# Layer 0's output begun inside the delta rule's last rounds, with GpSimd in the written order and shorter chains of the output norms

## The chip, the cores and the metric

The kernel runs on one core of a Trainium2 chip. The metric is the device time of one execution in microseconds (us). A core has five engines that work side by side: TensorE (PE in the profile; its weight loads are PEld), VectorE (DVE), ScalarE (ACT), GpSimd (POOL) and SyncE (SP), which starts most transfers. Each works through its own instructions in order and waits at an instruction for semaphores that others raise.

## The reference

The program is a backbone of two layers over 256 context rows and 512 latent rows of width 1024. Layer 0 is a gated DeltaNet in both directions, layer 1 an attention layer. The change concerns the end of layer 0. The delta rule goes through chunks of 64 rows:

```python
def step(s, xs):
    qk_i, qd_i, kd_i, u_i, w_i, gl_i = xs
    v_new = u_i - jnp.einsum('bhcd,bhde->bhce', w_i, s)
    o = jnp.einsum('bhcd,bhde->bhce', qd_i, s) + jnp.einsum('bhcs,bhse->bhce', qk_i, v_new)
    s = s * gl_i[..., None, None] + jnp.einsum('bhcd,bhce->bhde', kd_i, v_new)
    return s, o
```

and its output o (16 heads of 128) is normed, gated and multiplied with the output weights:

```python
def finish(o, z):
    b, h, l, dv = o.shape
    o = rms_norm(jnp.transpose(o, (0, 2, 1, 3)), o_norm_g).astype(z.dtype)
    return (o.reshape(b, l, DN_VAL_DIM) * jax.nn.silu(z)) @ w_out
```

A gated residual add follows, then layer 1, which begins with a norm of the rows h.

## The kernel before, in words

All 768 rows are six tiles of 128 (t = 0 to 5); O[t] holds the delta rule's output of a tile for 16 heads.

**The loop.** The delta rule is a loop of 50 rounds x over 48 updates: x // 4 is a step along the chunks, x % 4 a set of four heads. Round x issues products(x) (TensorE ks, L1065; VectorE r, L1068; ScalarE o, L1070; GpSimd's decay of the state S, L1073, twice, and on a tile's second visit its O += o, L1076), solve(x-1) (pr, L1090, and ScalarE's vn, L1092) and update(x-2) (pq, L1112; su, L1120; VectorE's O +=, L1123, and S +=). So three updates are on their way at any time. Steps before the last one make su; the last four updates (44 to 47) don't.

**The norms of O.** square_o (L896, ScalarE) sums the squares of a tile and head. scale_pieces is a generator: each send issues two or three small VectorE operations (L906 to L926) that make 1/sqrt with a corner of a PSUM bank as scratch, and its last pieces scale O by fo on GpSimd, four operations a tile (L932). In the loop the scratch is a corner of pq or a tile "room"; the generators for tiles 0 and 1 start at round 24, for tile 5 at 39.

**The output.** 32 units n (two groups of three tiles, 16 heads each). Unit n+2 is prepared while unit n is multiplied: three transposes of O into the PSUM tile pt (L980), the gate (L983, VectorE, times silu z), ScalarE's copy y0 = pt rounded (L985), VectorE's y1 = pt - y0 (L986). Then po of unit n: 18 matmuls, three tiles by two halves by three passes, y0 x woh, y0 x wol, y1 x woh (L1205). The output weights wo come by a transfer and are split in woh (ScalarE, L947) and wol = wo - woh (first half GpSimd L949, second half VectorE L951). There are two buffers for woh and wol, so the cast for unit n+2 waits for the last matmul of unit n. In units 0 to 9 ScalarE also squares O of tiles 4, 3 and 2 (five a unit), and the generators for these tiles start at units 4, 7 and 10, four sends a unit, behind the copy, with column 3 of pt as scratch.

**Behind group 0.** gated (L1214, VectorE) multiplies the accumulators by a gate; GpSimd adds the results to h (L1221) and ScalarE squares h (L1222), two each in units 16, 17 and 18. norms1 makes their 1/sqrt in unit 20 and normed (L1246, ScalarE) scales h in units 21 to 23. From unit 24 on u_block turns h for layer 1: transposes ht (L1255), one VectorE operation (L1257), ScalarE's copy and VectorE's difference uC (L1258, L1259). pt and ht share two PSUM banks, "tr".

**The order.** PE, DVE and ACT run in the order in which the program issues them (tc.manual_schedule). GpSimd is not in that list in the loop and the units, and a scheduler places its instructions. PSUM has eight banks: in the loop two each for ks, pr, pq and su; behind it two for "tr" and six for the accumulators.

Of the kernel before, what the change touches and what calls it, by code (L numbers as in the profile page):

```python
# [8 lines left out]
F32 = mybir.dt.float32  # L9
# [8 lines left out]
P = 128  # L18
# [79 lines left out]
def backbone(tc, a, out):  # L98
# [799 lines left out]
    def scale_pieces(t0, n):  # L898


        c = n * VH
        f, o_, y, w = (x[:, t0:t0 + n].rearrange("p t h -> p (t h)") for x in (fo, oss, oy, ow))
        r_ = rq[:, t0:t0 + n].rearrange("p t h -> p (t h)")
        by2 = lambda x: x.rearrange("p (h r) -> p h r", r=2)
        sp = (yield)[:, 0:c]
        V.tensor_copy(sp, o_)  # L906
        V.tensor_tensor(by2(sp), by2(sp), bcast(r_, 2, 2), ALU.mult)
        V.tensor_copy(w, sp)
        sp = (yield)[:, 0:c]
        V.tensor_copy(sp, w)  # L910
# [15 lines left out]
        V.tensor_tensor(by2(f), by2(sp), bcast(r_, 2, 2), ALU.mult)  # L926
        for t in range(t0, t0 + n):
            for q in range(4):
                if q % 2 == 0:
                    yield  # L930
                h = slice(4 * q, 4 * q + 4)
                G.tensor_tensor(O[t][:, h], O[t][:, h], bcast(fo[:, t, h], 2, P), ALU.mult)  # L932

# [38 lines left out]

    def out_y(n, pt=None):

        gi, h = units0[n]
        z = zs.pop(n)
        if pt is None:
            pt = ptr.tile([P, 4, P], F32, tag="tr", name=f"pt{h}_{gi}")
        for j, (t, off, st_) in enumerate(GROUPS[gi]):
            T.transpose(pt[:, j, :], O[t][:, h, :], ident)  # L980
        for j, (t, off, st_) in enumerate(GROUPS[gi]):
            pj = pt[:, j].rearrange("p (a k) -> p a k", a=2)
            V.scalar_tensor_tensor(pj, pj, og, raw(z, off, [[st_, 2], [1, 64]]), ALU.mult, ALU.mult)  # L983
        y = [fw.tile([P, 3, P], F32R, tag=f"y{i}", name=f"y{i}_{h}_{gi}", bufs=3) for i in range(2)]
        S.copy(y[0], pt[:, :3])  # L985
        V.tensor_tensor(y[1], pt[:, :3], y[0], ALU.subtract)  # L986
        ys[n] = y
        return pt

    with tc.tile_pool(name="psC", bufs=2, space=PSUM, reuse_waits="tile") as pcx:  # L990
# [59 lines left out]
        def products(x):  # L1050
# [8 lines left out]
            for j in range(2):  # L1059
                hh = 2 * p + j  # L1060
                ks = pcx.tile([P, 2, 2, P], F32, tag="ks", name=f"ks{x}_{j}", bufs=2)
                for w in range(2):
                    for d in range(2):
                        r0 = (visit ^ d) * 64
                        T.matmul(ks[r0:r0 + 64, w], kq[:, w, slot(hh), r0:r0 + 64], St[hh][:, d], start=True, stop=True)  # L1065
                h0 = 2 * slot(hh)
                for i in range(2):
                    V.scalar_tensor_tensor(r[:, 2 * j + i], ks[:, 0, i], negV[:, visit, t, h0 + i:h0 + i + 1], v[:, 2 * hh + i], ALU.mult, ALU.add)  # L1068
                for i in range(2):
                    S.activation(o[:, 2 * j + i], ks[:, 1, i], AF.Copy, scale=egV[:, visit, t, h0 + i:h0 + i + 1])  # L1070
                if s < 11:
                    g_ = glb[:, visit, :, t, h0:h0 + 2]
                    G.tensor_tensor(St[hh], St[hh], bcast(g_, 3, P), ALU.mult)  # L1073
# [27 lines left out]
        def update(x):  # L1101
# [11 lines left out]
            if s < 11:  # L1113
                su = pcx.tile([P, 2, 2, 2, P], F32, tag="su", name=f"su{x}", bufs=1)
# [29 lines left out]
        for _, g_ in chores:  # L1144
            next(g_)
        with tc.manual_schedule(engines={T.engine, V.engine, S.engine}):
            for x in range(50):
                if x < 48:
                    products(x)
                if 0 <= x - 1 < 48:  # L1150
                    solve(x - 1)
                if x == 49:
                    for h in range(2):
                        out_y(h, pcx.tile([P, 4, P], F32, tag="ks", name=f"pt{h}_0", bufs=2))
                if 0 <= x - 2 < 48:
# [5 lines left out]
                if x in (45, 46):  # L1161
                    out_load(x - 45)
                    out_weights(x - 45, False)
                    out_z(x - 45)
        for _, g_ in chores:
            for _ in g_:
                pass

    ch_c.__exit__(None, None, None)


    tr_c = tc.tile_pool(name="psT", bufs=2, space=PSUM, reuse_waits="tile")
    ptr = tr_c.__enter__()
    PASS = ((0, 0), (0, 1), (1, 0))
    SCALE = 128.0 ** -0.5
# [20 lines left out]
    ORDER = [t for g_ in GROUPS for t, _, _ in g_]  # L1196

    def products0(n, acc):

        gi, h = units0[n]  # L1200
        y, ww = ys.pop(n), weights.pop(n)
        for j in range(3):
            for nh in range(2):
                for x, (i, k) in enumerate(PASS):
                    T.matmul(acc[j][nh], y[i][:, j, :], ww[k][:, nh * 512:(nh + 1) * 512], start=h == 0 and x == 0, stop=h == VH - 1 and x == 2)  # L1205

# [29 lines left out]
    def norms1(gi, room_):  # L1236
# [12 lines left out]

    def u_block(k, j, tiles, dst):  # L1250

# [7 lines left out]
        V.tensor_tensor(dst[1][:, k], pv, dst[0][:, k], ALU.subtract)  # L1259
# [7 lines left out]
    for g_ in chores.values():  # L1267
        next(g_)
    squares = [(t, h) for t in (4, 3, 2) for h in range(VH)]
    late_adds = []  # L1270
    loads0 = {3: lambda: load_h(0), 5: lambda: load_h(1), 7: lambda: load_h(5), 9: lambda: dma(gate0[:, 0], gate_d[0][:, 0]), 11: lambda: dma(gate0[:, 1], gate_d[0][:, 1]), 13: lambda: load_h(4), 18: lambda: load_h(3), 20: lambda: load_h(2)}
    for n in range(len(units0)):
        gi, h = units0[n]
        if h == 0:
            acc = [[pf.tile([P, 512], F32, tag=f"po{j}{nh}", name=f"po{gi}{j}{nh}") for nh in range(2)] for j in range(3)]
# [508 lines left out]
```

## Time and profile before

| what | us |
|---|---|
| three runs of the kernel, median | 1248.55 |
| lowest and highest of them | 1247.85, 1249.84 |
| the profiled execution, whole time | 1247.08 |
| its span (first to last instruction) | 1245.3 |
| mean granted clock of TensorE | 0.977 |
| the delta rule's last products begin | 773.72 |
| first matmul of the output (po) | 783.48 |
| group 0's last unit ends, about | 862.7 |
| first transposes of h (ht) | 903.71 |

A row of the trace in order of time reads: start, duration, engine, line, operation, output <- inputs with their shapes, how many in a row (x8), and in brackets how long the engine was idle before it and what ended that. A row of a window reads: its bounds and length, the busy time of each engine (and instructions), the granted clock, the busy share of the DMA engines and GB/s. The line numbers are those of the kernel before; the profile calls a buffer by its name without the number.

### The profile page before, as it was taken

What the parts mean: (1) busy time and instruction counts of PE and PEld (TensorE: products, weight loads), DVE (VectorE), ACT (ScalarE), POOL (GpSimd) and SP (SyncE); (2) the same over time, 40 slices, a digit from 0 to 9 for tenths busy, and PEclk for the clock granted to TensorE, in tenths of its full rate; (3) what the DMA queues carried; (4) which work ended last, traced back from release to release, by engine and by line L of the source; (5) the groups of instructions that cost most, each with busy time, mean ns of one, the idle gap of its engine ahead of it and who ended that gap; (6) DMA issues with size and microseconds to landing.
All of it is one profiled execution on the core that took longest, in us unless ns stands there. A gap on an engine that the chain in (4) does not pass through costs nothing.

```text
span 1245.3 us, 28148 instructions
## 1 busy us (share of the span) xinstructions
PE 1151.1 (92%) x10755; PEld 925.9 (74%) x10755; DVE 833.3 (67%) x1884; ACT 724.4 (58%) x1934; POOL 601.2 (48%) x486
## 2 busy tenths in 40 slices
PE   3999999999789979899999999889999989999896
PEld 1776778888678868788666666768777778989784
DVE  2498666868688655575688888577666766556535
ACT  4544346665575767974689887543543246766621
POOL 0121123149999999700485598347455043140630
PEclk9999999999899989999999999999999999999998
DMA  9478965555435589555978855456744011111133
GB/s 316 159 222 268 297 216 165 149 143 187 127 98 158 175 247 273 191 193 184 274 213 241 236 159 156 159 170 194 208 161 136 18 51 52 35 34 52 59 103 93
DMA packets 165496, 204.56 MB, mean 164 GB/s; under 512 B 13393, under 2 KB 114930, under 8 KB 164594
## 3 DMA queue, kind: packets, MB, share of 16 engines
q1 hardware_dynamic: 146162, 193.10, 50.7%
q10 hardware_dynamic: 19200, 9.67, 2.6%
q8 instruction: 85, 1.39, 0.5%
q14 instruction: 49, 0.40, 0.1%
HBM read 161.96 MB, written 40.67 MB: 163 GB/s over the span
## 4 chain that ended last, share of the span: by engine, by line
PE 55%; DVE 13%; POOL 11%; ACT 7%; DMA 6%; issue 5%; SPq 2%; ACTq 0%; POOLq 0%; DVEq 0%
PE ks L1065 7%; PE g_z L414 6%; PE g_k L414 4%; PE g_q L414 4%; PE po L1205 4%; POOL X L755 4%; POOL tmp L754 3%; PE pg L1488 3%; PE su L1120 3%; PE po L1597 2%; PE pr L1090 2%; PE pso L1616 2%; PE pg L1534 2%; PE pa L245 2%; PE pq L1112 2%
## 5 line engine op out<-in xcount | busy, mean ns | idle before, releaser
L1073 POOL TENSOR_TENSOR S<-S,glb 128x512 f32<-128x512 f32 x88 | 90.1, 1046 | 112.8 <-PE ks L1065 112.6
L1205 PE MATMUL po<-woh,y 128*128 128x512 f32 x384 | 128.3, 402 | 1.0 <-DVE O L1123 0.8
L414 PE MATMUL g_v<-uh,wh 128*128 128x512 f32 (+1 forms) x256 | 91.2, 356 | 15.8 <-DVE sil_v L441 15.8
L755 POOL TENSOR_TENSOR X<-X,tmp 128x62 f32<-128x62 f32 (+15 forms) x93 | 95.7, 1029 | 6.5
L436 DVE SCALAR_TENSOR_TENSOR acc_v<-g_v,cwv,acc_v 128x510 f32<-128x510 f32 (+3 forms) x128 | 74.5, 609 | 33.4 <-ACT acc_v L433 32.0
L1065 PE MATMUL ks<-S,ckq 128*64 128x256 f32 x768 | 93.5, 385 | 3.1 <-ACT o L1070 2.5
L754 POOL TENSOR_TENSOR tmp<-L,X 128x62 f32<-128x62 f32 (+15 forms) x93 | 89.9, 967 | 6.9
L414 PE MATMUL g_z<-uh,wh 128*128 128x512 f32 (+1 forms) x256 | 88.4, 345 | 4.4 <-DVE sil_v L441 4.4
L414 PE MATMUL g_v<-ul,wh 128*128 128x512 f32 (+1 forms) x256 | 89.9, 351 | 0.0
L414 PE MATMUL g_v<-uh,wl 128*128 128x512 f32 (+1 forms) x256 | 89.2, 349 | 0.0
L414 PE MATMUL g_z<-ul,wh 128*128 128x512 f32 (+1 forms) x256 | 86.9, 340 | 0.0
L414 PE MATMUL g_z<-uh,wl 128*128 128x512 f32 (+1 forms) x256 | 86.8, 339 | 0.0
L949 POOL TENSOR_TENSOR wol<-wo,woh 128x512 fp32r<-128x512 f32 (+1 forms) x32 | 53.4, 1671 | 68.6 <-ACT woh L947 63.9
L1205 PEld LDWEIGHTS po<-woh,y 128*128 128x128 f32 x384 | 72.9, 190 | 16.4 <-DVE O L1123 1.2
L1205 PE MATMUL po<-wol,y 128*128 128x512 f32 x192 | 76.1, 396 | 7.6 <-POOL wol L949 7.6
L1065 PEld LDWEIGHTS ks<-S,ckq 128*64 128x64 f32 x768 | 50.7, 136 | 42.2 <-ACT o L1070 11.3
L211 POOL TENSOR_TENSOR wl_k<-w_k,wh_k 128x1024 fp32r<-128x1024 f32 x8 | 19.2, 2402 | 100.4 <-ACT wh_k L210 100.4
L414 PEld LDWEIGHTS g_v<-uh,wh 128*128 128x128 f32 x256 | 50.8, 198 | 22.6 <-DVE sil_v L441 16.5
L1580 DVE TENSOR_TENSOR pT<-pt,pT 128x384 fp32r<-128x384 f32 x64 | 33.3, 554 | 42.3 <-ACT pT L1579 42.3
L1138 DVE TENSOR_TENSOR S<-su,S 128x512 f32<-128x512 f32 x88 | 56.5, 684 | 4.3 <-PE su L1120 3.0
L1068 DVE SCALAR_TENSOR_TENSOR r<-ks,negV,cv 128x128 f32<-128x128 f32 x192 | 56.2, 344 | 4.1 <-PE ks L1065 3.3
L414 PEld LDWEIGHTS g_z<-uh,wh 128*128 128x128 f32 x256 | 48.9, 191 | 10.4 <-DVE sil_v L441 5.3
(417 smaller groups left out, 3378.0 us busy)
## 6 DMA issues: line engine op xcount, KB each, us to landing
aw<-in_ada_w SPq DMA_DIRECT2D x24, 1024.0 KB, 7.8
w<-in_dn_w_in SPq DMA_DIRECT2D x40, 512.0 KB, 4.4
wo<-in_dn_w_out SPq DMA_DIRECT2D x32, 512.0 KB, 3.5
cv<-v_d SPq DMA_DIRECT2D x80, 128.0 KB, 5.3
df<-gc_d SPq DMA_DIRECT2D x48, 128.0 KB, 2.8
z_d<-zs SPq DMA_DIRECT2D x16, 384.0 KB, 5.1
v_d<-vt ACTq DMA_DIRECT2D x16, 384.0 KB, 4.4
t_d<-Tt SPq DMA_DIRECT2D x6, 1024.0 KB, 5.1
```

Source lines behind the costliest of these rows:

```text
L414: mm = T.matmul(pg_[:m, :n], w[:, k, :m], u[:, k, c0:c0 + n], start=k == 0 and n_ == 0, stop=k == KT - 1 and n_ == 2)
L436: V.scalar_tensor_tensor(acc[:, c0 + lo:c0 + hi], ps[:, lo + j - 2:hi + j - 2], cwv[:, j, ct:ct + 1], acc[:, c0 + lo:c0 + hi], ALU.mult, A ...
L754: E.tensor_tensor(tv, bcast(L[:, :, j + 1:, j], 3, j + 1), bcast(X[:, :, j, 0:j + 1], 2, n), ALU.mult)
L755: E.tensor_tensor(X[:, :, j + 1:, 0:j + 1], X[:, :, j + 1:, 0:j + 1], tv, ALU.subtract)
L949: G.tensor_tensor(wl[:, :c], w[:, :c], wh[:, :c], ALU.subtract)
L1065: T.matmul(ks[r0:r0 + 64, w], kq[:, w, slot(hh), r0:r0 + 64], St[hh][:, d], start=True, stop=True)
L1068: V.scalar_tensor_tensor(r[:, 2 * j + i], ks[:, 0, i], negV[:, visit, t, h0 + i:h0 + i + 1], v[:, 2 * hh + i], ALU.mult, ALU.add)
L1073: G.tensor_tensor(St[hh], St[hh], bcast(g_, 3, P), ALU.mult)
L1120: T.matmul(su[c0:c0 + 64, d ^ j, j], kt[r0:r0 + 64, 4 * j + p, c0:c0 + 64], vd[r0:r0 + 64, 2 * j:2 * j + 2], start=True, stop=True)
L1138: V.tensor_tensor(St[hh], raw(sj, 0, [[512 - 1024 * j, 2], [P, 2], [1, P]]), St[hh], ALU.add)
L1205: T.matmul(acc[j][nh], y[i][:, j, :], ww[k][:, nh * 512:(nh + 1) * 512], start=h == 0 and x == 0, stop=h == VH - 1 and x == 2)
L1488: T.matmul(pgq, uL[i][:, k, t * P:(t + 1) * P], wq[j][:, k], start=k == 0 and n_ == 0, stop=k == KT - 1 and n_ == 2)
```

## The change

Four things. The lines of the changed kernel are other numbers for the same statements (L929 the scaling of O, L947 wol, L1102 O += o, L1242 the addition to h).

1. The generators of the norms issue 16 small operations in place of 27, in 5 sends in place of 12. Their scalings are put on a list, and scale_o(n) issues the next n of it at written places: one or two in nine of the rounds 30 to 47, then one behind the weights of each unit, two from unit 12 on.
2. GpSimd joins the written order in the loop and the units.
3. ks moves into the pool of pt ("tr"), and su, the scratch tile and the accumulators of a group's first tile share another. So unit 0's transposes and gate stand in round 48 ahead of the last solve, unit 1's behind update(46), and the first tile's six matmuls of units 0 and 1 behind the last update. The weights of the first two units are loaded two rounds earlier and split one round earlier or at the same place.
4. out_y and u_block are split in two. In the units with small operations, these (two sends a unit) now stand between gate and copy; in the units from 24 on the transposes of pt and ht stand together, then both VectorE operations, then copy and difference of each. norms1 for group 0 becomes a generator in units 19 and 20.

The diff, cut:

```diff
@@ scale_pieces
-                if q % 2 == 0:
-                    yield
-                h = slice(4 * q, 4 * q + 4)
-                G.tensor_tensor(O[t][:, h], O[t][:, h], bcast(fo[:, t, h], 2, P), ALU.mult)
+                pool_todo.append((t, q))
+
+    def scale_o(n):
+        for t, q in pool_todo[:n]:
+            h = slice(4 * q, 4 * q + 4)
+            G.tensor_tensor(O[t][:, h], O[t][:, h], bcast(fo[:, t, h], 2, P), ALU.mult)
+        del pool_todo[:n]
...
@@ the loop
-        with tc.manual_schedule(engines={T.engine, V.engine, S.engine}):
+        with tc.manual_schedule(engines={T.engine, V.engine, S.engine, G.engine}):
             for x in range(50):
                 if x < 48:
                     products(x)
+                if x == 48:
+                    out_first(0)
                 if 0 <= x - 1 < 48:
                     solve(x - 1)
-                if x == 49:
-                    for h in range(2):
-                        out_y(h, pcx.tile([P, 4, P], F32, tag="ks", name=f"pt{h}_0", bufs=2))
                 if 0 <= x - 2 < 48:
                     update(x - 2)
+                if x == 48:
+                    out_second(0)
+                    out_first(1)
+                if x == 49:
+                    out_second(1)
+                    acc0 = first_acc(0)
+                    for n in range(2):
+                        products0(n, [acc0], (0,))
...
+                scale_o({30: 2, 31: 2, 34: 1, 37: 1, 40: 1, 43: 1, 45: 1, 46: 2, 47: 1}.get(x, 0))
...
@@ the units
-        pt = out_y(n + 2) if n + 2 < len(units0) else None
+        pt = out_first(n + 2) if n + 2 < len(units0) else None
+        if n >= 24:
+            u_first(n - 24, 1, (0, 1))
+        if n == 19:
+            next(chores[19])
         for x in [x for x in chores if x <= n]:
-            for _ in range(4):
+            for _ in range(2):
                 try:
                     chores[x].send(pt[:, 3])
...
+        if n + 2 < len(units0):
+            out_second(n + 2)
+        if n >= 24:
+            u_second(n - 24, 1, uC)
...
-        products0(n, acc)
+        products0(n, acc, (1, 2) if n < 2 else (0, 1, 2))
...
         if n + 2 < len(units0):
             out_weights(n + 2)
+        scale_o(2 if n >= 12 else 1)
         if n in (16, 17, 18):
             for x in range(2):
                 added(*late_adds.pop(0), G)
```

GpSimd from the weights of unit 13 to those of unit 20, before (wol_0 is group 0, wol_1 group 1, which begins with unit 16; O_7091 and O_7090 are tiles 3 and 2; L1221 is the addition to h):

```order
L949 TENSOR_TENSOR wol_0_10926<-wo_0_10834,woh_0_10925 128x512
L949 TENSOR_TENSOR wol_0_10974<-wo_0_10883,woh_0_10973 128x512
L932 TENSOR_TENSOR O_7090<-O_7090,fo 128x512 x4
L949 TENSOR_TENSOR wol_0_11015<-wo_0_10933,woh_0_11014 128x512
L949 TENSOR_TENSOR wol_1_11054<-wo_1_10981,woh_1_11053 128x512
L1221 TENSOR_TENSOR h_10296<-h_10296,gy_0_11092 128x512
L949 TENSOR_TENSOR wol_1_11105<-wo_1_11022,woh_1_11104 128x512
L1221 TENSOR_TENSOR h_10296<-h_10296,gy_1_11094 128x512
L1221 TENSOR_TENSOR h_10297<-h_10297,gy_0_11096 128x512
...
L949 TENSOR_TENSOR wol_1_11150<-wo_1_11061,woh_1_11149 128x512
L949 TENSOR_TENSOR wol_1_11193<-wo_1_11118,woh_1_11192 128x512
```

The same place now:

```order
L929 TENSOR_TENSOR O_7091<-O_7091,fo 128x512 x2
L947 TENSOR_TENSOR wol_0_10966<-wo_0_10887,woh_0_10965 128x512
L929 TENSOR_TENSOR O_7090<-O_7090,fo 128x512 x2
L947 TENSOR_TENSOR wol_1_11007<-wo_1_10932,woh_1_11006 128x512
L929 TENSOR_TENSOR O_7090<-O_7090,fo 128x512 x2
L947 TENSOR_TENSOR wol_1_11060<-wo_1_10975,woh_1_11059 128x512
L947 TENSOR_TENSOR wol_1_11104<-wo_1_11016,woh_1_11103 128x512
L1242 TENSOR_TENSOR h_10292<-h_10292,gy_0_11047 128x512
L1242 TENSOR_TENSOR h_10292<-h_10292,gy_1_11049 128x512
L947 TENSOR_TENSOR wol_1_11147<-wo_1_11072,woh_1_11146 128x512
L1242 TENSOR_TENSOR h_10293<-h_10293,gy_0_11051 128x512
L1242 TENSOR_TENSOR h_10293<-h_10293,gy_1_11053 128x512
```

The scalings of tile 2 stood as four ahead of wol of unit 15 and now stand as two behind it and two behind that of unit 16. The first addition to h stood behind wol of unit 16 and five more behind that of unit 17; now two stand behind wol of 18, 19 and 20 each.

VectorE in unit 4, where the norm of tile 4 begins, before (unit 6 is prepared; pt_0_10511 is its tile):

```order
L983 SCALAR_TENSOR_TENSOR pt_0_10511<-pt_0_10511,og,z_0_10460 128x128 x3
L986 TENSOR_TENSOR y_6_0_10519<-pt_0_10511,y_6_0_10518 128x384
L906 COPY pt_0_10511<-oss 128x16
L907 TENSOR_TENSOR pt_0_10511<-pt_0_10511,rq 128x16
...
L919 TENSOR_TENSOR ow<-pt_0_10511,oy 128x16
L951 TENSOR_TENSOR wol_0_10556<-wo_0_10463,woh_0_10555 128x512
```

And now:

```order
L982 SCALAR_TENSOR_TENSOR pt_0_10493<-pt_0_10493,og,z_0_10442 128x128 x3
L906 TENSOR_TENSOR pt_0_10493<-oss,rq 128x16
L907 TENSOR_TENSOR pt_0_10493<-pt_0_10493,rq 128x16
L908 TENSOR_SCALAR fo<-pt_0_10493 128x16
L910 COPY pt_0_10493<-fo 128x16
L911 TENSOR_SCALAR pt_0_10493<-pt_0_10493 128x16
L912 TENSOR_SCALAR oy<-pt_0_10493 128x16
L992 TENSOR_TENSOR y_6_0_10507<-pt_0_10493,y_6_0_10506 128x384
L949 TENSOR_TENSOR wol_0_10534<-wo_0_10445,woh_0_10533 128x512
```

Ten small operations stood behind the difference y1; now six stand between the gate and y1, and so ahead of ScalarE's copy, which y1 needs.

TensorE at the end of the loop now (pr and pq belong to the last solves and updates; pt_0_10216 and pt_0_10248 are units 0 and 1):

```order
L1138 MATMUL pq_10204<-vn_10153,cQK_9976 64x128 x8
L979 MATMUL pt_0_10216<-ident,O_7088 128x128
L979 MATMUL pt_0_10216<-ident,O_7089 128x128
L979 MATMUL pt_0_10216<-ident,O_7093 128x128
L1116 MATMUL pr_10223<-r_10172,cT_9975 64x128 x8
L1138 MATMUL pq_10234<-vn_10202,cQK_9976 64x128 x8
L979 MATMUL pt_0_10248<-ident,O_7088 128x128
...
L1138 MATMUL pq_10255<-vn_10232,cQK_9976 64x128 x8
L1004 MATMUL po_10269<-woh_0_10060,y_0_0_10244 128x512
```

Before, both units' transposes stood between the last two pq, and the first po behind unit 2's transposes.

More of the change, by code (lines that the diff above doesn't have):

```diff
@@ L987, in out_y, with products0, first_acc @@
         ys[n] = y
-        return pt
+    PASS = ((0, 0), (0, 1), (1, 0))
+    def products0(n, acc, js):
+        gi, h = units0[n]
+        y, ww = ys[n], weights[n]
+        for j in js:
+            for nh in range(2):
+                for x, (i, k) in enumerate(PASS):
+                    T.matmul(acc[j][nh], y[i][:, j, :], ww[k][:, nh * 512:(nh + 1) * 512], start=h == 0 and x == 0, stop=h == VH - 1 and x == 2)
+    tr_c = tc.tile_pool(name="psT", bufs=2, space=PSUM, reuse_waits="tile")
+    ptr = tr_c.__enter__()
+    psU_c = tc.tile_pool(name="psU", bufs=1, space=PSUM, reuse_waits="tile")
+    pU = psU_c.__enter__()
+    def first_acc(gi):
+        x = pU.tile([P, 2, 512], F32, tag="su", name=f"po{gi}0")
+        return [x[:, nh] for nh in range(2)]
     with tc.tile_pool(name="psC", bufs=2, space=PSUM, reuse_waits="tile") as pcx:
@@ L1060, in products @@
                 hh = 2 * p + j
-                ks = pcx.tile([P, 2, 2, P], F32, tag="ks", name=f"ks{x}_{j}", bufs=2)
+                ks = ptr.tile([P, 2, 2, P], F32, tag="tr", name=f"ks{x}_{j}")
                 for w in range(2):
@@ L1113, in update @@
             if s < 11:
-                su = pcx.tile([P, 2, 2, 2, P], F32, tag="su", name=f"su{x}", bufs=1)
+                su = pU.tile([P, 2, 2, 2, P], F32, tag="su", name=f"su{x}")
                 for j in range(2):
@@ L1160, in backbone @@
                         squares = squares[1:]
[L1161 to L1167, printed above, removed]
+                scale_o({30: 2, 31: 2, 34: 1, 37: 1, 40: 1, 43: 1, 45: 1, 46: 2, 47: 1}.get(x, 0))
+                if x in (43, 45):
+                    out_load((x - 43) // 2)
+                    out_z((x - 43) // 2)
+                if x in (44, 46):
+                    out_weights((x - 44) // 2, False)
+        assert not chores and not pool_todo, (chores, pool_todo)
     ch_c.__exit__(None, None, None)
-    tr_c = tc.tile_pool(name="psT", bufs=2, space=PSUM, reuse_waits="tile")
-    ptr = tr_c.__enter__()
-    PASS = ((0, 0), (0, 1), (1, 0))
     SCALE = 128.0 ** -0.5
@@ L1196, in backbone @@
     ORDER = [t for g_ in GROUPS for t, _, _ in g_]
[L1198 to L1205, printed above, removed]
     def gated(gi, acc):
@@ L1240, in norms1, with norm_pieces @@
         rsqrt(r, 1.0 / D, room=room_)
+    def norm_pieces(gi):
+        r = hr[:, 3 * gi:3 * gi + 3]
+        y = hpool.tile([P, 3], F32, tag="hy", name=f"hy{gi}")
+        V.tensor_tensor(r, hsq[:, 3 * gi:3 * gi + 3, 0], hsq[:, 3 * gi:3 * gi + 3, 1], ALU.add)
+        sp = (yield)[:, 0:3]
+        V.tensor_scalar(sp, r, 1.0 / D, EPS, ALU.mult, ALU.add)
+        V.tensor_copy(r, sp)
+        V.tensor_single_scalar(sp.bitcast(I32), sp.bitcast(I32), 1, ALU.logical_shift_right)
+        V.tensor_scalar(y.bitcast(I32), sp.bitcast(I32), -1.0, float(0x5F3759DF), ALU.mult, ALU.add)
+        for i in range(3):
+            sp = (yield)[:, 0:3]
+            V.scalar_tensor_tensor(sp, y, -0.5, y, ALU.mult, ALU.mult)
+            V.tensor_tensor(sp, sp, r, ALU.mult)
+            V.scalar_tensor_tensor(r if i == 2 else y, sp, 1.5, y, ALU.add, ALU.mult)
     def normed(t, E):
@@ L1248, in normed, with u_first @@
             E.tensor_scalar(h_t[t], h_t[t], r, None, ALU.mult)
-    def u_block(k, j, tiles, dst):
+    turned_u = {}
+    def u_first(k, j, tiles):
         n = len(tiles) * P
@@ L1268, in backbone @@
         next(g_)
+    chores[19] = norm_pieces(0)
     squares = [(t, h) for t in (4, 3, 2) for h in range(VH)]
@@ L1274, in backbone @@
         if h == 0:
-            acc = [[pf.tile([P, 512], F32, tag=f"po{j}{nh}", name=f"po{gi}{j}{nh}") for nh in range(2)] for j in range(3)]
+            acc = [acc0 if gi == 0 else first_acc(1)] + [[pf.tile([P, 512], F32, tag=f"po{j}{nh}", name=f"po{gi}{j}{nh}") for nh in range(2)] for j in (1, 2)]
         if n + 3 < len(units0):
```

47 lines of the change are left out of this document (25 added, 22 removed).

## The prediction, made before the changed kernel ran

> **What bounds the kernel now.** I read the page first, for who is busy; then the instructions of TensorE in order of time, with what ended each idle stretch, from the last rounds of the delta rule to the end of layer 0's output; then those of GpSimd, VectorE and ScalarE beside each idle stretch; last the busy time by windows. The page:
>
> ```profile
> span 1245.3 us, 28148 instructions
> PE 1151.1 (92%) x10755; PEld 925.9 (74%) x10755; DVE 833.3 (67%) x1884; ACT 724.4 (58%) x1934; POOL 601.2 (48%) x486
> L1205 PE MATMUL po<-wol,y 128*128 128x512 f32 x192 | 76.1, 396 | 7.6 <-POOL wol L949 7.6
> ```
>
> TensorE is busy for 92% of the span, and the change removes no matmul. All it can win is idle time of TensorE, 94.2 us in the whole span, and it touches only the stretch from the delta rule's 30th round to unit 30 of the output. In that stretch the idle of before stands in few rows. GpSimd, then TensorE, in the loop:
>
> ```profile
> 731.60 8.04 POOL L932 TENSOR_TENSOR O<-O,fo 128x512 f32<-128x512 f32 x8
> 739.59 2.06 POOL L1073 TENSOR_TENSOR S<-S,glb 128x512 f32<-128x512 f32 x2
> 741.59 1.27 POOL L1076 TENSOR_TENSOR O<-O,o 128x512 f32<-128x512 f32 x1
> ...
> 743.58 1.95 PE L1065 MATMUL ks<-S,ckq 128*64 128x256 f32 x16 [1.81 <-ACT o L1070]
> 747.35 1.95 PE L1065 MATMUL ks<-S,ckq 128*64 128x256 f32 x16
> 773.72 1.95 PE L1065 MATMUL ks<-S,ckq 128*64 128x256 f32 x16 [0.73 <-ACT o L1070]
> ```
>
> A round takes 3.77 us (743.58 to 747.35). The eight scalings of O in one lump hold GpSimd for 8.04 us, and TensorE waits 1.81 us behind them; the last products wait 0.73. TensorE at the end of the loop and through the first units:
>
> ```profile
> 777.57 0.67 PE L1090 MATMUL pr<-r,cT 64*64 64x128 f32 x16 [0.87 <-ACT vn L1092]
> 780.33 0.66 PE L980 MATMUL pt<-ident,O 128*128 128x128 f32 x4 [1.28 <-POOL O L932]
> 783.21 0.52 PE L980 MATMUL pt<-ident,O 128*128 128x128 f32 x3 [1.63 <-DVE y L986]
> 785.92 0.50 PE L1205 MATMUL po<-woh,y 128*128 128x512 f32 x1 [0.80 <-DVE O L1123]
> ...
> 793.24 0.49 PE L980 MATMUL pt<-ident,O 128*128 128x128 f32 x3
> 797.71 0.49 PE L980 MATMUL pt<-ident,O 128*128 128x128 f32 x3
> ...
> 816.46 0.50 PE L1205 MATMUL po<-wol,y 128*128 128x512 f32 x1 [0.16 <-POOL wol L949]
> 826.07 0.80 PE L1205 MATMUL po<-wol,y 128*128 128x512 f32 x1 [4.53 <-POOL wol L949]
> 826.66 1.05 PE L1205 MATMUL po<-woh,y 128*128 128x512 f32 x2
> ```
>
> A unit of TensorE alone is 4.47 us long (793.24 to 797.71). What TensorE then waits for is the second part of the split weights, wol: GpSimd did four scalings of O before it. Behind the 4.53 us of idle the matmuls are slower, and the windows put it down to the clock (PEclk, behind the busy times):
>
> ```profile
> 821.00:826.00 5.00, 0.50 (x1) 0.19 (x1) 4.00 (x14) 2.88 (x12) 5.00 (x6) 0.97 0.49 120
> 826.00:830.00 4.00, 3.93 (x11) 3.15 (x12) 3.29 (x7) 1.03 (x6) 1.27 (x2) 0.60 0.64 205
> ```
>
> At a granted clock of 0.60 for 4 us the stretch lost some 1.4 us ((1 - 0.60) x 4 = 1.6 at most).
>
> **The change, part by part** (against the profiled execution of 1247.08 us, whose span is 1245.3; the median of the three runs is 1248.55, which is 1.47 more, and I add that at the end).
>
> *1. The scalings spread over rounds 30 to 47, shorter chains.* One scaling is 1.0 us (8.04 / 8). A round with a pair of S (2.06) and one O (1.27) has 0.45 left of 3.77, so a scaling makes GpSimd 0.6 late once, and two rounds later it has caught up; the lump of 8.04 cost 1.81, so 1.0 is covered. The 1.81 goes. The 0.73 goes too, as the small operations that stood there are done earlier. **-2.5**; if the cover fails at each of the four later places, 4 x 0.6 = 2.4 comes back.
>
> *2. The output begins in the last rounds.* Unit 0's transposes now stand ahead of the last solve, the lump of four scalings that they waited for (POOL O L932) is spread, and twelve matmuls of units 0 and 1 need only the first tile of each, so they stand where TensorE waited for y and O. The four idles of the tail, 0.87 + 1.28 + 1.63 + 0.80 = 4.58, are filled but for about 0.2 (unit 0 still waits for the last O of VectorE): **-4.4**. The new accumulators stand where su did; su is unused in the last rounds, so nothing waits for them.
>
> *3. Small operations between the gate and ScalarE's copy.* In the units up to 13 the work runs in a ring: wol, gate, copy of y, five squares, cast woh, wol again. VectorE's wol and the chain:
>
> ```profile
> 799.62 0.69 DVE L951 TENSOR_TENSOR wol<-wo,woh 128x512 fp32r<-128x512 f32 x1 [1.85 <-ACT woh L947]
> 804.37 0.69 DVE L951 TENSOR_TENSOR wol<-wo,woh 128x512 fp32r<-128x512 f32 x1 [1.85 <-ACT woh L947]
> 807.32 0.18 DVE L906 COPY pt<-oss 128x16 f32<-128x16 f32 x1
> 807.53 0.18 DVE L907 TENSOR_TENSOR pt<-pt,rq 128x16 f32<-128x16 f32 x1
> ...
> 809.32 1.69 DVE L951 TENSOR_TENSOR wol<-wo,woh 128x512 fp32r<-128x512 f32 x1
> 815.26 1.68 DVE L951 TENSOR_TENSOR wol<-wo,woh 128x512 fp32r<-128x512 f32 x1
> ```
>
> The ring is 4.75 us (799.62 to 804.37), 0.28 over TensorE's 4.47, and 5.94 where ten small operations stand ahead of wol (809.32 to 815.26). Now six or three of them stand ahead of the copy, in every round of a chain: 0.21 each (807.32 to 807.53), so 1.28 or 0.64 more. At unit 2 the ring leads: TensorE would reach that wol 15.7 us after the last products began (773.72; before it was 20.1, half a us behind 793.24, less the 4.4 of step 2), and by the durations above it is there at about 14.5 (an estimate), so 1.2 ahead. At 0.28 a unit that is 0.3 when unit 6 comes. The waits of units 6 to 13 come out as 1.2, 1.6, 0.9, 1.6, 1.5, 0.3, 0.1, 0.1 (the squares end at unit 9, which shortens the ring), in all 7.3. Before, this stretch lost 0.16 + 4.53 + 1.4 = 6.1, and that goes, since a single scaling now stands behind each wol. **+1.2**. The copy reads other columns of the tile than the small operations write, and no row of before shows such a pair side by side; if the copy did not wait for them, 1.28 would fit into VectorE's 1.85 of idle, and only 9 x 0.28 - 1.2 = 1.3 of waits would be left: -4.8. Taken is the first, since both work on one tile in one bank and waits are kept by tile. [...]
>
> *4. Unit 16 waits for GpSimd.* Before, the scalings of O of tile 2 ran as a lump of four ahead of wol of unit 15. Now the first two stand right behind that wol, and the third transpose of unit 16, ahead of unit 14's matmuls, needs the first. The wol waits for its cast, and the cast for the matmuls of unit 13, which give its buffer free. Rows of before for each link:
>
> ```profile
> 858.55 1.05 ACT L947 CAST woh<-wo 128x1024 fp32r<-128x1024 f32 x1 [0.40 <-PE po L1205]
> ...
> 859.68 1.80 POOL L949 TENSOR_TENSOR wol<-wo,woh 128x512 fp32r<-128x512 f32 x1 [1.00 <-ACT woh L947]
> ```
>
> From the last matmul: about 0.2 to the cast, 1.05, wol 1.80 (1.28 where VectorE does its half at another time), scaling 1.0: **+4.0**, between 3.4 and 4.3. There is no work for TensorE beside it.
>
> *5. The additions of h in pairs behind wol of units 18, 19, 20.* Before, they ran as 1 and 5, and ScalarE's squares of h followed late:
>
> ```profile
> 863.23 1.30 POOL L1221 TENSOR_TENSOR h<-h,gy 128x512 f32<-128x512 f32 x1 [1.74 <-DVE gy L1214]
> 865.74 7.20 POOL L1221 TENSOR_TENSOR h<-h,gy 128x512 f32<-128x512 f32 x5
> ...
> 874.22 0.50 PE L1205 MATMUL po<-wol,y 128*128 128x512 f32 x1 [1.56 <-POOL wol L949]
> 898.23 0.50 PE L1205 MATMUL po<-wol,y 128*128 128x512 f32 x1 [1.35 <-POOL wol L949]
> ```
>
> In the new order a ring closes: cast woh 1.04, wol 1.85, two additions 2.56 (2 x 1.28), the second square 0.7, copy of y 0.4, cast again: 6.6 us, against 4.47 for TensorE. It turns three times, from wol of unit 18 to 21. Lead and the eight small operations of the norm (8 x 0.23) counted, TensorE waits about 1.5 at unit 19, 2.1 at 20, 4.0 at 21 and 0.3 at 22: 7.9. Before lost 1.56 + 1.35 and, counted from unit to unit, 0.7 more: 3.6. **+4.3**, between +2.5 (squares and additions overlap better) and +6.
>
> *6. u_block split in two.* Its four waits in the units 24 to 29:
>
> ```profile
> 903.71 0.42 PE L1255 MATMUL ht<-ident,h 128*128 128x128 f32 x2 [0.96 <-PE pt L980]
> 909.42 0.41 PE L1255 MATMUL ht<-ident,h 128*128 128x128 f32 x2 [0.80 <-DVE uC L1259]
> ...
> 919.48 0.41 PE L1255 MATMUL ht<-ident,h 128*128 128x128 f32 x2 [0.44 <-DVE uC L1259]
> 929.54 0.41 PE L1255 MATMUL ht<-ident,h 128*128 128x128 f32 x2 [0.45 <-DVE uC L1259]
> ```
>
> The two chains on the two banks now run beside each other, and the sum, 0.96 + 0.80 + 0.44 + 0.45 = 2.65, goes: **-2.6**, at least -1. The rest of the kernel keeps its order but for a few matmuls near its end: 0, bounded by 0.5 both ways.
>
> *7. The clock.* The one idle of 4.53 was followed by 1.4 of loss; those of 1.81 and 1.56 were not. The waits of unit 16 (4.0) and of unit 21 (4.0, broken by one matmul) lie nearer to 4.53: I count three quarters of 1.4 for the first and half for the second, **+1.8**. [...]
>
> Sum: -2.5 - 4.4 + 1.2 + 4.0 + 4.3 - 2.6 + 1.8 = +1.8, so 1248.9 for the profiled execution and **1250.4** beside the median.
>
> **The rivals.** About 0.2%, 2.5 us, is what a measurement of this kernel can tell from no change: 1246.05 to 1251.05 counts as the same.
>
> *The ring through the additions runs slower than 6.6* (slower). If both squares of h follow the additions (1.6 in place of 0.7), it is 7.5, three turns cost 2.7 more, and the wait of unit 21 passes 4.53 and surely takes the clock (+0.7): 1250.4 + 3.4 = 1253.8. For it speaks that ScalarE's two squares always ran back to back; against, that the first may start a whole addition earlier. It decides from a ring of 6.8 on. Chance 0.35.
>
> *The copy does not wait for the small operations* (faster): term 3 is -4.8 in place of +1.2, 1250.4 - 6.0 = 1244.4. For it: different columns; against: one tile. Chance 0.15.
>
> [...] Chance 0.13.
>
> **How the numbers follow.** My forecast, gains of 9.5 given back by new waits, has 0.37. The range takes in both faster rivals' centres but not their tails, and the slower one's: 1243.5 to 1254.5. Faster 0.28 (the two faster rivals), same 0.37, slower 0.35.
>
> **What the profile after would show.** Right: no lump of eight scalings and no wait of 1.81 in the loop; the first matmul of po inside the last solve; waits of 1 to 1.6 in the units 6 to 10 with ScalarE's copy behind the last small operation; one wait of about 4 ahead of the third transpose of unit 16, released by GpSimd; three growing waits at units 19 to 21; no ht row with a wait over 0.3. Wrong: if units 6 to 10 run at 4.5 to 4.8 us, the copy is free and term 3 falls; if unit 16's transposes start at once, term 4 falls; if the units 19 to 21 wait for under 4 in all, term 5 falls; if the tail of the loop keeps over 2 of its 4.58, term 2 falls and the kernel is slower than I say.

## The result, and the profile after

The changed kernel takes 1255.62 us (median of 6 runs, 1254.3 to 1256.54), the kernel before 1248.2 beside it (6 runs): ratio 1.0058, 95% interval 1.0046 to 1.0069. It is slower by 0.6%, 5.2 over the forecast and 1.1 above the range. The profiled execution took 1256.36 with a span of 1254.5, 9.2 more than the span of before.

TensorE's instructions that stand in both kernels cut the span into stretches. Their starts after the change (ks of updates 36 and 47; first transposes of units 4, 16, 18 and 26; the eighth ht; the first transpose of attention):

```profile
729.92 0.44 PE L1091 MATMUL ks<-S,ckq 128*64 128x256 f32 x2
772.42 0.44 PE L1091 MATMUL ks<-S,ckq 128*64 128x256 f32 x2
788.01 0.27 PE L979 MATMUL pt<-ident,O 128*128 128x128 f32 x1
853.46 0.27 PE L979 MATMUL pt<-ident,O 128*128 128x128 f32 x1
869.83 0.27 PE L979 MATMUL pt<-ident,O 128*128 128x128 f32 x1
912.50 0.27 PE L979 MATMUL pt<-ident,O 128*128 128x128 f32 x1
945.97 0.27 PE L1294 MATMUL ht<-ident,h 128*128 128x128 f32 x1
1033.71 0.27 PE L1635 MATMUL pt<-ident,pr 128*128 128x128 f32 x1
```

The same instructions stood at 730.38, 773.72, 793.24, 853.81, 862.75, 902.26, 938.24 and 1023.24 before. The differences, beside what the terms of the prediction say:

| stretch | before | after | change | foretold (step) |
|---|---|---|---|---|
| up to ks 36 | 730.38 | 729.92 | -0.5 | 0 |
| ks 36 to ks 47 | 43.34 | 42.50 | -0.8 | -2.5 (1) |
| ks 47 to unit 4 | 19.52 | 15.59 | -3.9 | -4.4 (2) |
| unit 4 to 16 | 60.57 | 65.45 | +4.9 | +1.2 (3) |
| unit 16 to 18 | 8.94 | 16.37 | +7.4 | +5.05 (4, part of 7) |
| unit 18 to 26 | 39.51 | 42.67 | +3.2 | +5.0 (5, part of 7) |
| unit 26 to the eighth ht | 35.98 | 33.47 | -2.5 | -2.6 (6) |
| to attention | 85.00 | 87.74 | +2.7 | 0 |
| to the end | 222.06 | 220.79 | -1.3 | 0 |

The sum is +9.2, foretold +1.8. The stretch to attention holds no edit; there TensorE's granted clock was 0.79 in the 24 us from 961.8 on, and over all twelve profiled kernels of this study that stretch took 83.8 to 88.3 with no edit in it. The medians stand 7.4 apart, so about 2 of the 9.2 belong to the two profiled executions: that of before lay 1.1 under its median, that of after 0.7 over.

The larger waits of TensorE after the change, in the stretches that the prediction spoke of (all rows between them are left out):

```profile
768.34 1.09 PE L1146 MATMUL su<-vd,ckt 64*64 64x256 f32 x16 [0.74 <-DVE S L1164]
...
807.47 0.50 PE L1004 MATMUL po<-wol,y 128*128 128x512 f32 x1 [0.87 <-POOL wol L947]
813.52 0.50 PE L1004 MATMUL po<-wol,y 128*128 128x512 f32 x1 [1.29 <-POOL wol L947]
...
824.01 0.50 PE L1004 MATMUL po<-woh,y 128*128 128x512 f32 x1 [0.60 <-ACT woh L945]
825.86 0.69 PE L1004 MATMUL po<-wol,y 128*128 128x512 f32 x1 [1.34 <-POOL wol L947]
...
858.95 0.48 PE L979 MATMUL pt<-ident,O 128*128 128x128 f32 x1 [5.12 <-POOL O L929]
891.33 0.51 PE L1004 MATMUL po<-wol,y 128*128 128x512 f32 x1 [1.40 <-POOL wol L947]
897.30 0.52 PE L979 MATMUL pt<-ident,O 128*128 128x128 f32 x3 [1.82 <-DVE y L992]
899.46 0.50 PE L1004 MATMUL po<-wol,y 128*128 128x512 f32 x1 [1.40 <-POOL wol L947]
```

The lump of eight scalings and its wait of 1.81 are gone, and of the tail's four waits two of 0.40 and 0.50 are left. In their place stand two waits at su (0.30 and 0.74), waits of 0.6 to 1.4 for wol, once for woh, in every unit from 6 to 13, one of 5.12 at unit 16 and three in units 20 and 21.

VectorE beside them, at the weights of units 6 to 9, shows something that no step of the prediction had:

```profile
805.60 0.69 DVE L949 TENSOR_TENSOR wol<-wo,woh 128x512 fp32r<-128x512 f32 x1 [1.85 <-ACT woh L945]
...
811.65 0.69 DVE L949 TENSOR_TENSOR wol<-wo,woh 128x512 fp32r<-128x512 f32 x1 [1.85 <-ACT woh L945]
...
817.06 0.69 DVE L949 TENSOR_TENSOR wol<-wo,woh 128x512 fp32r<-128x512 f32 x1 [1.85 <-ACT woh L945]
817.67 1.14 DVE L982 SCALAR_TENSOR_TENSOR pt<-pt,og,z 128x128 f32<-128x128 f32 x3
818.84 1.07 DVE L906 TENSOR_TENSOR pt<-oss,rq 128x16 f32<-128x16 f32 x1
819.95 0.18 DVE L907 TENSOR_TENSOR pt<-pt,rq 128x16 f32<-128x16 f32 x1
...
823.99 0.69 DVE L949 TENSOR_TENSOR wol<-wo,woh 128x512 fp32r<-128x512 f32 x1 [1.85 <-ACT woh L945]
```

and GpSimd at the same time:

```profile
818.84 1.04 POOL L929 TENSOR_TENSOR O<-O,fo 128x512 f32<-128x512 f32 x1
```

The ring from wol to wol is 6.05 with six small operations in it (805.60 to 811.65), as foretold (4.75 + 1.28). Then it is 6.93 (817.06 to 823.99): the first small operation lasts 1.07 in place of 0.18, from the start of GpSimd's scaling to its end. It happens in six units, and it is always the first of the chain, which reads both operands from SBUF: oss and rq, or oy twice. Its neighbours read one operand from PSUM and last 0.18. In the loop it happens twice, for 1.27 and 1.19, beside GpSimd's additions of 1.27. Before the change each chain copied one operand to PSUM first, and none of its small operations from 700 us on lasted over 0.20.

### The profile page after: what moved, and what is told of

It is laid out like the page before. It is cut to its first block, busy times and chain, and to the rows that moved or that the text cites. A ratio compares the mean times of both kernels' runs of the same rounds, so it can differ in the third digit from the quotient of the medians.

```text
span 1254.5 us, 28104 instructions
## 1 busy us (share of the span) xinstructions
PE 1158.2 (92%) x10755; PEld 930.2 (74%) x10755; DVE 826.2 (66%) x1836; ACT 724.7 (58%) x1934; POOL 602.6 (48%) x486
## 5 line engine op out<-in xcount | busy, mean ns | idle before, releaser
L947 POOL TENSOR_TENSOR wol<-wo,woh 128x512 fp32r<-128x512 f32 (+1 forms) x32 | 57.7, 1804 | 83.4 <-ACT woh L945 70.5
```

Of the source, the lines that this page charges most:

```text
L947: G.tensor_tensor(wl[:, :c], w[:, :c], wh[:, :c], ALU.subtract)
```

## The experiments

Each was timed in 5 rounds against the kernel before, whose median moved between 1249.3 and 1250.3 in these sessions; so ratios are compared (0.001 of the ratio is 1.25 us).

**Small operations with one operand in PSUM.**

```diff
-        V.tensor_tensor(by2(sp), by2(o_), bcast(r_, 2, 2), ALU.mult)
+        V.tensor_copy(sp, o_)
+        V.tensor_tensor(by2(sp), by2(sp), bcast(r_, 2, 2), ALU.mult)
...
-            V.scalar_tensor_tensor(sp, y, -0.5, y, ALU.mult, ALU.mult)
+            V.tensor_scalar(sp, y, -0.5, None, ALU.mult)
+            V.tensor_tensor(sp, sp, y, ALU.mult)
```

> The changed kernel, but the small operations of the output norms that read two operands from SBUF (the first product, the half square, the last product) take a copy or a scaled copy in PSUM first, as before the change: 21 small operations a tile in place of 16, everything else as changed. Theory A (such an operation waits for GpSimd's running instruction, which is why one in three lasts 1.07 to 1.27 us in place of 0.18): all small operations last 0.18, the ring of units 8 to 13 loses 0.89 and gains 0.21 a unit, the waits of 0.30 and 0.74 in the loop go; the median falls from 1255.6 by 4 to 6, to 1249.5 to 1251.5. Rival (the first small operation behind the gate waits for the scaling of O whatever it reads): the 1.07 stays, the median is 1255.5 to 1257.

Measured: 1255.6, ratio 1.0049 (1.0037 to 1.0061): no gain clear of the noise. But all small operations last 0.18, here with a scaling of GpSimd started within 0.01 us of the first:

```profile
818.89 0.18 DVE L906 COPY pt<-oss 128x16 f32<-128x16 f32 x1
819.11 0.18 DVE L907 TENSOR_TENSOR pt<-pt,rq 128x16 f32<-128x16 f32 x1
```

```profile
818.88 1.04 POOL L932 TENSOR_TENSOR O<-O,fo 128x512 f32<-128x512 f32 x1
```

So the wait is a matter of operands (0.18 with one in PSUM, 1.07 with both in SBUF, each beside a scaling of 1.04), and theory A's mechanism holds; its price failed. The stretch ks 36 to ks 47 won 0.9 (41.6 in place of 42.5), but units 4 to 16 only 1.3 (64.2): the five operations more of each tile stand in the ring as well, where turns of 6.05 now take up to 6.47 and turns of 6.93 up to 6.46. At su a wait of 0.53 is left, behind the small operations that stand ahead of S in one round. In the profiled execution the gain was given back from unit 18 to 26 (45.2 in place of 42.7), where the clock fell to 0.50 for 5 us (two matmuls in a row took 1.05 in place of 0.62, from 897.89 to 902.59).

**Scalings of tile 2 one unit earlier.**

```diff
-        scale_o(2 if n >= 12 else 1)
+        scale_o(2)
```

> The changed kernel, but each unit issues up to two scalings of O from the first, so those of tile 2 stand behind the weights of units 14 and 15 and not 15 and 16. Theory B (unit 16's transposes wait for the chain matmuls of unit 13, cast, wol, scaling): the wait of 5.12 at unit 16 and the slow clock behind it go, 6 to 7 in all, median 1248.5 to 1250. Rival (the scalings in pairs hold GpSimd and VectorE twice as long at units 4 to 10, and that takes it back): under 3 won, median 1252.5 or more.

Measured: 1247.15, ratio 0.9983 (0.9968 to 0.9998). Theory B holds: the wait of 5.12 is 0.57, and the clock behind it stays up. From 853 to 865, the changed kernel and this one:

```profile
853.00:859.00 6.00, 0.89 (x6) 0.52 (x5) 2.72 (x6) 1.42 (x2) 6.00 (x6) 0.81 0.75 204
859.00:865.00 6.00, 6.00 (x18) 4.76 (x19) 1.64 (x4) 0.48 (x1) 0.89 (x1) 0.62 0.36 113
```

```profile
853.00:859.00 6.00, 5.43 (x28) 4.25 (x27) 3.56 (x7) 1.90 (x3) 6.00 (x6) 1.00 0.84 231
859.00:865.00 6.00, 5.36 (x27) 4.28 (x26) 4.22 (x9) 2.58 (x3) 2.35 (x3) 1.00 0.58 192
```

TensorE was busy for 0.89 of 6 us and then ran at a clock of 0.62; now 5.43 and 1.00. Unit 16 to 18 takes 9.7 in place of 16.4. By the ratio the gain is 9.4, more than the 6 to 7 foretold: units 4 to 16 take 63.4 in place of 65.4 as well, while 18 to 26 takes 44.2 in place of 42.7, since the clock fell behind the waits there (0.76 from 892 to 899, with 1.05 for two matmuls in a row in place of 0.62).

**Copy ahead of the small operations.**

```diff
-        for x in [x for x in chores if x <= n]:
...
         if n + 2 < len(units0):
             out_second(n + 2)
         if n >= 24:
             u_second(n - 24, 1, uC)
+        for x in [x for x in chores if x <= n]:
```

> The changed kernel, but ScalarE's copy and VectorE's difference of y stand ahead of the unit's small operations again, as before the change. Theory C (the copy is held by the small operations on the same tile, so they lie in the ring): the waits of units 8 to 13, 7.9 in all, and the slow clock at unit 10 mostly go, 5 to 8 won, median 1248 to 1251. Rival (VectorE is the ring there and the order of its own instructions doesn't matter): under 2 won, median 1253.6 or more.

Measured: 1246.31, ratio 0.9969 (0.9956 to 0.9982): by the ratio 11 won, where 5 to 8 were foretold. Units 4 to 16 as one window, the changed kernel and this one:

```profile
788.00:853.50 65.50, 57.60 (x254) 45.10 (x253) 39.80 (x107) 28.81 (x107) 26.61 (x18) 0.97 0.57 176
```

```profile
789.50:844.20 54.70, 54.64 (x254) 43.98 (x253) 36.42 (x105) 28.81 (x107) 26.99 (x19) 1.00 0.69 212
```

TensorE has no idle left there (54.64 of 54.70): the small operations, 1.07 or 0.18, lie beside ScalarE's squares. 10.8 went there, and 2.2 came back from unit 18 to 26, where the norm of h still waits for the squares and now holds the tile that unit 23's transposes need (a wait of 2.35 at 888.12, ended by VectorE's hy, L1277).

**The same order, scratch in the other bank.**

```diff
+        corner = pt if n else None
         pt = out_first(n + 2) if n + 2 < len(units0) else None
...
-                    chores[x].send(pt[:, 3])
+                    chores[x].send(corner[:, 3])
```

> The changed kernel, every instruction in its order, but the small operations of unit n use a corner of the tile of unit n+1 (whose copy is done) as scratch and not of unit n+2, so the copy and they lie in two banks. Theory C (it is the shared bank that holds ScalarE's copy): the copy follows the gate at once, units 4 to 16 fall from 65.4 to under 60, 4 to 7 won, median 1248.5 to 1251.5. Rival (VectorE's difference of y, which stands behind the small operations, is what delays TensorE): under 2 won, median over 1253.6.

Measured: 1247.54, ratio 0.9986 (0.9971 to 1.0002). Theory C holds: with every instruction in its place ScalarE's copy no longer waits for the last small operation (L917, in the changed kernel, first row) but for the gate (this kernel, second row), and units 4 to 16 fall from 65.4 to 56.7. By the ratio 9 are won, over the 4 to 7 foretold. Two limits of this run: the other corner lies in another tile as well as in another bank, so it doesn't tell which of the two the wait is kept by; and the first small operation now begins 0.1 us ahead of GpSimd's scaling and is not held for 1.07, so not all of the gain is the copy's. One such first operation, begun at 820.17, takes 0.22; the next that reads oy twice begins at 820.85, inside the scaling (820.31 to 821.35), and takes 0.54, to that scaling's end.

```profile
828.00 0.48 ACT L991 CAST y<-pt 128x384 fp32r<-128x384 f32 x1 [4.04 <-DVE oy L917]
```

```profile
820.35 0.48 ACT L991 CAST y<-pt 128x384 fp32r<-128x384 f32 x1 [1.87 <-DVE pt L982]
```

A part is lost again further on: the norm of h now holds the tile that unit 22's transposes need, TensorE waits 7.03 there, and the stretch from 18 to 26 takes 46.2.

**Additions to h ahead of wol.**

```diff
+        if n in (16, 17, 18):
+            for t, nh, gy in late_adds[:2]:
+                c = slice(nh * 512, (nh + 1) * 512)
+                G.tensor_tensor(h_t[t][:, c], h_t[t][:, c], gy, ALU.add)
         if n + 2 < len(units0):
             out_weights(n + 2)
...
-                added(*late_adds.pop(0), G)
+                added(*late_adds.pop(0), None)
```

> The changed kernel, but in units 16 to 18 the two additions to h stand ahead of the unit's wol on GpSimd; ScalarE's squares stay where they are. Theory D (a ring wol, additions, squares, copy, cast, wol of 6.5 us holds units 19 to 22): the waits of 1.40, 1.82 and 1.40 fall to under 1.5 in all, 3 to 4 won, median 1251.5 to 1252.5. Rival (the additions only move their 2.5 ahead of wol, which TensorE then waits for as it did before the change): under 1 won, median 1254.6 or more.

(`added` with None leaves the addition out and keeps the square.) Measured: 1246.74, ratio 0.9975 (0.9963 to 0.9987), over twice what was foretold. Theory D holds in kind. In the changed kernel the ring stands in GpSimd's rows, 6.49 from wol to wol; the window is that from unit 18 to 26:

```profile
876.53 1.80 POOL L947 TENSOR_TENSOR wol<-wo,woh 128x512 fp32r<-128x512 f32 x1 [4.04 <-ACT woh L945]
878.29 2.54 POOL L1242 TENSOR_TENSOR h<-h,gy 128x512 f32<-128x512 f32 x2
883.02 1.79 POOL L947 TENSOR_TENSOR wol<-wo,woh 128x512 fp32r<-128x512 f32 x1 [2.20 <-issue]
...
889.51 1.77 POOL L947 TENSOR_TENSOR wol<-wo,woh 128x512 fp32r<-128x512 f32 x1 [2.20 <-issue]
```

```profile
869.80:912.50 42.70, 37.26 (x169) 29.17 (x168) 22.79 (x59) 19.00 (x31) 24.21 (x16) 1.00 0.60 183
```

With the additions first the ring is open, and TensorE waits 0.64 in the whole stretch:

```profile
868.60:905.20 36.60, 35.96 (x170) 29.32 (x169) 23.90 (x60) 20.25 (x33) 26.01 (x17) 1.00 0.71 216
```

That is 6.1, and 1.1 more goes at the first ht, which no longer waits 0.88. I had counted only the idle of the three waits over 1 us, 4.6 in all. The waits cost more here than their idle shows: the same matmuls were busy for 37.26 with the waits and for 35.96 without, both at a granted clock of 1.00.

**GpSimd free in the units.** The list of engines of the units' written order is the old one, `{T.engine, V.engine, S.engine}`; in the loop GpSimd stays in it.

> The changed kernel, but GpSimd is in the written order in the loop only; in the units the scheduler places it, which puts the scalings back into lumps of four and the additions to h back to one and five. Theory (the two waits behind unit 14 come from the written order): 16 to 18 falls from 16.4 to about 9 and 18 to 26 from 42.7 to 39.5 or less; the lump of tile 4 costs about 2 to 4 at units 7 to 9; median 1246 to 1250. Rival (they come from the longer ring and not from GpSimd's order): over 1253.

Measured: 1245.41, ratio 0.997 (0.9953 to 0.9987). Unit 18 to 26 falls to 37.8 and 16 to 18 to 12.6, not to 9: the lump for tile 2 leaves a wait of 1.80 there, with a clock of 0.86 in the window. So the written order of GpSimd in the units cost all of the loss from 18 to 26, but only half of that from 16 to 18 (3.8 of 7.4). Units 4 to 16 take 63.7, less than the 65.4 of the changed kernel, though the lumps of four stand there again and were foretold to cost 2 to 4.

**The loop's part alone.** The same, with copy first and u_block unsplit.

> The same, and the copy ahead of the small operations and u_block unsplit as before the change: the part in the loop alone (spread scalings, output begun in the last rounds) with the shorter chains. Theory (the loop and its tail win 0.8 and 3.9 as the trace of the changed kernel has it, and nothing takes it back): 4 to 6 under the kernel before, 1243 to 1245.5. Rival (the units, begun earlier, only wait longer for ScalarE's ring): within 2 of the kernel before.

Measured: 1241.9, ratio 0.9933 (0.9911 to 0.9955), more than foretold. Loop and tail win 0.8 and 3.9 again (42.5 and 15.6); units 4 to 16 take 60.3 and 16 to 18 9.5, about as before; 18 to 26 takes 37.8, 1.8 less than before, and 26 to the eighth ht 34.5, 1.5 less. Why these last two are better with the shorter chains wasn't tried by itself. Against the run before this one, 16 to 18 falls by another 3.1, so most of the other half of its loss goes with the place of the copy.

**u_block's split alone**, in the kernel before.

> The kernel before, with only out_y of units 26 to 31 and u_block split and interleaved as in the change. Theory (its four waits of 2.65 in all go): 2 to 3 under the kernel before, ratio 0.998. Rival (the split moves VectorE's work so that wol comes later and TensorE waits there): no difference.

Measured: 1246.92, ratio 0.9973 (0.9957 to 0.9989), as foretold; unit 26 to the eighth ht takes 33.6 in place of 36.0. But only three of the four waits went: the first, 0.96 in the kernel before, is 1.00 here.

**Three places mended together, and all four.**

> The changed kernel with three of its places undone at once: copy and difference of y ahead of the small operations, the scalings of tile 2 one unit earlier, the additions to h ahead of wol. If the three waits are separate (the sum of the stages of the three single runs): units 4 to 16 take 54.6 us, 16 to 18 9.7, 18 to 26 36.6, all else as changed, 16 under the kernel before: 1232 to 1234. Rival (TensorE, come earlier to unit 16, 19 or 23, waits there for the same chains by another link): over 1238.

> The same three and, as a fourth, the small operations with one operand in PSUM (21 in place of 16). Theory A, second form (the wait of a two-SBUF operation for GpSimd is real, and its removal was worth nothing only because the five operations more stood in the ring): the loop wins 0.9 again, and the total is 0.5 to 2 under that of the three. Rival (behind the copy nothing waits for the small operations): within 0.5 of the three.

Measured: three 1234.57, ratio 0.9855 (0.9829 to 0.9881); four 1231.64, ratio 0.9843 (0.9818 to 0.9868). The waits are separate: the three give 55.8, 9.8 and 36.6 for the three stretches (54.6, 9.7 and 36.6 as the sum of the single runs). All four leave almost nothing idle from unit 4 to 26:

```profile
788.00:842.70 54.70, 54.61 (x253) 43.93 (x252) 37.97 (x122) 28.86 (x107) 29.41 (x21) 1.00 0.70 214
842.70:851.90 9.20, 9.09 (x43) 7.30 (x42) 5.77 (x14) 3.44 (x5) 7.03 (x6) 1.00 0.62 179
851.90:888.50 36.60, 35.96 (x169) 29.31 (x168) 23.97 (x60) 20.61 (x33) 25.41 (x16) 1.00 0.71 217
```

Between three and four the loop's stretch is 42.5 against 41.6, as theory A in its second form has it. The totals differ by 2.9, but their intervals overlap; how much of that the operands are worth is not settled. The version with all four beats the kernel before by 1.6%.

## Why the prediction was wrong, step by step

1. *Scalings spread* (-2.5, measured -0.8). The wait of 1.81 went as said. The step failed where it put the 0.73 and the small operations at nothing: with fewer sends more of them stand in one round, and two lasted 1.27 and 1.19 us beside GpSimd's additions to O (1.27 each, from 752.66 and 764.41).

```profile
752.71 1.27 DVE L906 TENSOR_TENSOR pq<-oss,rq 128x16 f32<-128x16 f32 x1
...
764.53 1.19 DVE L915 SCALAR_TENSOR_TENSOR pq<-oy 128x16 f32<-128x16 f32 x1
```

VectorE's S then comes late and su waits 0.30 and 0.74; the two rounds take 4.34 and 5.05 in place of 3.77, 1.8 more in all. One operand in PSUM took back 0.9 of it; the other half stays, behind the many small operations that stand ahead of S in one round.

2. *Early begin* (-4.4, measured -3.9): right. Waits of 0.40 and 0.50 are left; the first po ran behind the last update, not inside the last solve as I wrote.

3. *Small operations ahead of the copy* (+1.2, measured +4.9). The mechanism was right: the ring of 6.03 was 6.05, the copy waits for the small operations, and scratch in another tile and bank frees it. The step failed in the size of the waits. With the copy first, where TensorE has next to no idle, the stretch takes 54.6. So it lost 5.9 before, foretold 6.1, and 10.8 after, foretold 7.3. The window of before:

```profile
793.20:853.80 60.60, 55.81 (x253) 44.95 (x252) 43.25 (x134) 28.73 (x105) 28.06 (x21) 0.97 0.62 193
```

What the step left out is the hold of 0.89 (1.07 in place of 0.18) in six turns of the ring, those to the wol of units 9 to 14: turns counted at 6.03 took 6.93, and units 11 to 13, put at 0.3, 0.1 and 0.1 of wait, waited 0.97, 0.76 and 0.74. I had taken 0.21 for every operation from rows of the old chain, whose operands were others. How much of the missing 3.5 is the hold by itself was not measured, since the version with one operand in PSUM has more small operations (64.2).

The slow clock in unit 9 is no part of it, though TensorE's busy time rose with it. The kernel with the additions first has the same order of instructions up to unit 16, keeps the full clock in the whole stretch, and takes the same 65.45:

```profile
787.30:852.75 65.45, 56.22 (x254) 43.98 (x253) 39.77 (x107) 28.80 (x107) 26.59 (x18) 1.00 0.57 176
```

There unit 9 is shorter (6.88 in place of 8.53), but TensorE then waits 0.60 and 1.34 in unit 10, where the changed kernel, come later, waits 0.61. Units 9 and 10 together take 13.85 there and 13.88 in the changed kernel: the slow matmuls only filled a time in which TensorE would have waited for the ring.

The hold is in the traces: the first small operation, with two inputs in SBUF, lasted 1.07 beside GpSimd's scaling of 1.04, and 0.18 with an operand in PSUM; I had not asked of the new forms where they read from. The kernel before already showed it: VectorE's wol, with both inputs in SBUF, lasted 0.69 at 804.37, where it began 0.05 ahead of GpSimd's, and 1.69 at 809.32, where it began 0.14 behind GpSimd's of 1.28. That the copy waits for the small operations was a choice between two values in the prediction, which no run showed then; the runs now show the copy behind the last of them (idle 4.04, ended by L917), and behind the gate (1.87) with the scratch elsewhere. No run here parts the bank from the tile.

4. *Unit 16* (+4.0, measured wait 5.12). The chain was right; missing was what stands ahead of it, 1.1: the last wol could not begin until two scalings of tile 3 were done (0.5), and its cast stood behind a late copy (0.6).

```profile
854.20 2.04 POOL L929 TENSOR_TENSOR O<-O,fo 128x512 f32<-128x512 f32 x2
856.19 1.71 POOL L947 TENSOR_TENSOR wol<-wo,woh 128x512 fp32r<-128x512 f32 x1
857.86 2.03 POOL L929 TENSOR_TENSOR O<-O,fo 128x512 f32<-128x512 f32 x2
```

5. *The ring through the additions* (+4.3, measured +3.2, no clock lost): right in mechanism and in the turn, 6.49 against 6.6. The two losses were both put too high: with the ring open the stretch takes 36.6, so it lost 2.9 before (3.6 foretold) and 6.1 after (7.9 foretold), and the waits, put at 1.5, 2.1, 4.0 and 0.3 in units 19 to 22, came as 1.40 in unit 20 and 1.82 and 1.40 in unit 21. That the difference is near is in part luck. The slower rival said 7.5 a turn and fell, though its direction came true.

6. *u_block* (-2.6, measured -2.5): the size came true by luck. Three of the four waits went, 1.69 of idle, and each cost more than its idle; the first stayed (0.96 before, 0.88 after), against the sign of no ht row over 0.3.

7. *Clock* (+1.8). Behind unit 16 it cost 2.1, twice what was counted (6.43 from 858.95 to the next transposes, 4.28 with the scalings one unit earlier). At unit 21 it cost nothing in this execution, which is luck: in the runs with the scalings one unit earlier and with one operand in PSUM the same two waits, 1.8 and 1.4, were followed by slow matmuls, and that unit took 7.75 and 8.81 in place of 6.16.

So the mechanisms of steps 2 to 5 were there, and most of that of step 6, and the sum failed in 1, 3 and 4: by 1.7 for small operations in the loop, half of it held by GpSimd; by 3.7 in step 3, where the ring cost 10.8 and not 7.3; and by 2.4 at unit 16, 1.1 of them for what stood ahead in GpSimd's queue and 1.1 for the clock. From unit 18 to 26 it was 1.8 better than foretold.

## What to carry to other kernels

Price a shortened chain by the operands of its new instructions, not by the old instruction's time: a form that saves an instruction by reading both operands from SBUF can wait for a whole instruction of GpSimd (here 1.07 beside a scaling of 1.04, in place of 0.18). When an engine joins a written order, draw the ring that each of its places closes (who waits for it, what it waits for) and move what closes a ring one unit earlier; here three moved places were worth 2% together (ratio 1.0058 to 0.9855). Small work that shares a PSUM tile and bank with something urgent belongs behind it (here that won 10.8 us from unit 4 to 16). And look whether a slow clock lies on the longest path before putting a price on it (here units 9 and 10 took 13.88 with it and 13.85 without).

## What the runs showed of the hardware that I had not expected

In these runs, whether the clock fell was not a matter of one idle's length alone. In unit 9 of the changed kernel two waits, 0.60 and 1.34, with one matmul between them, were followed by slow matmuls:

```profile
826.35 1.05 PE L1004 MATMUL po<-woh,y 128*128 128x512 f32 x2
```

From the transposes of unit 11 to those of 12 the granted clock is 0.80. The kernel with the additions first has the same waits there, 0.55 and 1.35, and a granted clock of 1.00: the same span takes 6.88 (822.25 to 829.13) where the changed kernel takes 8.53 (822.92 to 831.45). As step 3 shows, the difference was gone one unit later. So the same waits were followed by slow matmuls in one execution and not in the other, as those of 1.8 and 1.4 in step 7, where the prediction had counted by the length of one idle. What else decides it was not shown.
